# Attention outputs kept once and split on return, returns on another queue, and a tile's finish moved: a decoder layer on one core

## The chip, the cores and the metric

The kernel runs on one core of one Trainium2 chip. It is one launch, in fp32 at its inputs and outputs. The metric is the device time of that launch in microseconds (us), as the median of its runs; lower is better. PE is TensorE (the matrix engine), DVE is VectorE, ACT is ScalarE, POOL is GpSimd, SP is SyncE, which here only issues transfers.

## The reference

One decoder layer: 512 tokens, width 2048, 16 query heads of 128 in 4 key/value groups, a feed-forward width of 5632.

```python
hn = rmsnorm(x, mix_norm_g)
h  = x + nsa_mixer(hn, ...)                       # attention in three branches
h  = h + swiglu(rmsnorm(h, ffn_norm_g), ffn_w_in, ffn_w_out)
return rmsnorm(h, final_norm_g)

# nsa_mixer, for each head:
proj = hn @ w_in                                  # q, and k and v for three branches, and gates
s_c  = q @ kcc.T + bias;  o_c = softmax(s_c) @ vcc    # 31 compressed keys (an MLP over 32-token blocks)
s_s  = q @ k_sel.T + bias; o_s = softmax(s_s) @ v_sel # chosen blocks of 64 keys
s_w  = q @ k_win.T + bias; o_w = softmax(s_w) @ v_win # window of 512
o    = gate_c * o_c + gate_s * o_s + gate_w * o_w
return concat(o) @ w_out
```

All softmaxes are causal. With 512 tokens there are only 8 blocks and up to 16 may be chosen, so the chosen branch covers every earlier key, and the window covers them too.

## The kernel before

Every fp32 product is made of three products of rounded pieces: a value is kept as a high piece (ACT copies it to the rounded type) and a low piece (DVE subtracts the high piece from the value). `three` (lines 266 to 269) issues high x high, high x low and low x high; which of L267, L268 and L269 a row has tells which of the three it is.

**Weights.** The class `Weights` brings them as granules of 128x1024. `load` (L81) issues the transfer into one of three buffers `raw`; `split` makes `whi` (ACT, L97) and `wlo` (DVE, L98); `take` hands out a granule and keeps three more split ahead. `W.queue` is POOL's queue while attention runs, and SP's before and behind it.

**Stages.** Up to about 200 us the kernel normalises the input, projects the first keys, values and queries and builds the compressed keys. From 200 to 705 us attention runs. Behind it come the rest of the output projection, the second norm and the feed-forward network to the end of the span at 2136 us.

**Attention** is a loop over 16 heads (h), of 12 steps (i) each, written out by hand; each engine executes its instructions in the order in which this loop issues them. Four kinds of work are interleaved:

- `scores(h+1, t)`, at i = 2, 5, 8 and 11 for the token tiles t = 3, 2, 1, 0 of the next head: PE's products into `s`, DVE's addition of the bias with a running minimum (L791, three per tile), ACT's exponentials (L793).
- `finish(h+1, t)`, at i = 3, 6, 9 and at step 0 of the next head: DVE scales the probabilities by gate over sum (reciprocal L798, products L805) and transposes them in blocks of 32 (L806); SP issues four transfers `d_p<-p` to DRAM (L808).
- `fetch(t)`: SP brings the turned probabilities back, `ptr<-d_p` (L812). It stands at i = 8 for tiles 3 and 2, and at steps 0 and 3 of the next head for tiles 1 and 0.
- `turn(h, b, kt)`, at steps 0 to 8, splits one piece of the fetched probabilities into `pth` (ACT, L829) and `ptl` (DVE, L833; L831 for the compressed branch). `values` two steps later multiplies it by the values into `o` (L267 to L269; L844 for the compressed branch, at step 10).

`head_out`, at step 10, splits `o` into `of0` and `of1` and stores both pieces in DRAM for heads 0 to 11, two transfers `d_o<-of`; heads 12 to 15 are split straight into `hn_h` and `hn_l`. These two tiles hold the normalised input until the last projection has read it, and take the heads' outputs then.

**The dense stream** fills PE between these: `dense` yields projections of queries (`qpair`), keys and values for later heads, and then four `partial` products of the first twelve heads' outputs with `w_out`, each ending in a sum with the input (`stage<-in_x`, L702) that goes to DRAM (`d_h<-stage`, L718). Each yield stands for 6 products and counts as 650 ns. `pump(h, step)` advances the stream until its count has reached a goal for this step:

```python
goal = 20800 * min(at, 13) + 18300 * max(at - 13, 0)
```

During the last query pair, `reload_o` (L694 to L697) brings the twelve heads' outputs back into `hn_h` and `hn_l`: six transfers of 1 MB on SP's queue, two for each four heads, as each quarter of the normalised input has been read. The partial products read them as they are; a later stage multiplies the rest of `w_out` with all sixteen heads.

Of the kernel before, what the change touches and what calls it, by code (L numbers as in the profile page):

```python
# [10 lines left out]
F32 = mybir.dt.float32  # L11
# [162 lines left out]
def nsa_block(ctx: ExitStack, tc: tile.TileContext, x, rel_bias, mix_g, ffn_g, fin_g, w_in, w_out,  # L174
# [21 lines left out]
    d_t = dram.tile([H, UL], F32, name="d_t")  # L196
    d_u = dram.tile([128, H * UL], F32, name="d_u")
    d_c = dram.tile([H, 16 * CL], F32, name="d_c")
    d_o = dram.tile([12, 2, 128, S], F32, name="d_o")
    d_h = dram.tile([S, 256 * N_SPILL], F32, name="d_h")  # L200
    d_r = dram.tile([NT, 128, D], F32, name="d_r")
    d_a = dram.tile([NF // 2, 128, 2 * S], F32, name="d_a")
# [87 lines left out]
    def split_from(psum_ap, hi, lo, scale=None):  # L290
        if scale is None:
            act(hi, psum_ap, AF.Copy)
            dve.tensor_tensor(lo, psum_ap, hi.bitcast(F32), op=OP.subtract)
        else:
            act(hi, psum_ap, AF.Copy, scale=scale)
            dve.scalar_tensor_tensor(lo, psum_ap, scale, hi.bitcast(F32), op0=OP.mult, op1=OP.subtract)
# [333 lines left out]
    with ExitStack() as st2:  # L630
# [24 lines left out]
        def qpair(h0):  # L655
            ps = proj2()
            end = q_out(ps, h0)
            for i in range(4):
                yield from ws(ps, i, W.take(), end=end)
                if h0 == H - 2 and i < 3:  # L660
                    reload_o(i)
            done["n"] += 1
            yield None

# [27 lines left out]
            yield None  # L692

        def reload_o(i):  # L694
            for part, t in enumerate((hn_h, hn_l)):
                nc.sync.dma_start(t[:, 4 * i:4 * i + 4].bitcast(F32),
                                  d_o[4 * i:4 * i + 4, part].rearrange("h p s -> p h s"))  # L697

        def partial(cb):
            st = stage_tile().rearrange("p (t c) -> p t c", t=NT)  # L700
            c = slice(256 * cb, 256 * (cb + 1))
            nc.sync.dma_start(st, x[:, c].rearrange("(t p) c -> p t c", p=128))  # L702
            ps = [p.rearrange("p (t c) -> p t c", t=2) for p in proj2()]
            for i in range(3):
                w = W.take()
                for t in range(NT):
                    if i == 2 and t == 2:
                        W.ahead(3)
                    for k in range(4):
                        h = 4 * i + k  # L710
                        three(ps[t // 2][:, t % 2], hn_h[:, h, tok(t)], hn_l[:, h, tok(t)], w[0][:, k], w[1][:, k],
                              h == 0 and t % 2 == 0, h == 11)
                        if k % 2:
                            yield 650
                    if i == 2 and t % 2:
                        b = t // 2
                        dve.tensor_tensor(st[:, 2 * b:2 * b + 2], st[:, 2 * b:2 * b + 2], ps[b], op=OP.add)
            nc.sync.dma_start(d_h[:, c].rearrange("(t p) c -> p t c", p=128), st)  # L718
            done["n"] += 1
            yield None  # L720

# [13 lines left out]

        def pump(h, step):
            at = h + (step + 4) / STEPS
            goal = 20800 * min(at, 13) + 18300 * max(at - 13, 0)
            while done["ns"] < goal:
                c = next(stream, "end")  # L740
                if c == "end":
                    return
                done["ns"] += c or 0
# [52 lines left out]
        def finish(h, t):  # L796
            r = HS[h]["sm"][:, t]
            dve.reciprocal(r, r)  # L798
            dve.tensor_mul(r, r, gates[:, t, h])
            for i, p in enumerate(HS[h].pop(t)):  # L800
                o = p
                if not i:
                    o = P[t][:, :3, runs[t] - 32:]
                    p = CX[t].unsqueeze(1).to_broadcast([128, 3, 32])
                dve.tensor_scalar(o, p, r[:, i:i + 1], None, op0=OP.mult)  # L805
            dve.transpose(P[t], P[t])  # L806
            for i in range(4):
                nc.sync.dma_start(d_p[t][:, :, i].rearrange("j a r -> a j r"), P[t][32 * i:32 * (i + 1)])  # L808

        def fetch(t):  # L810

            nc.sync.dma_start(PT[:, :, PT_STEP * t:PT_STEP * t + runs[t]], d_p[t].rearrange("j a i r -> (j a) i r"))  # L812
# [6 lines left out]
        def turn(h, b, kt):  # L819
            n = S - 128 * kt  # L820
            th = ap_.tile([128, 512], F32R, name="pth", bufs=3)
            tl = ap_.tile([128, 512], F32R, name="ptl")
            rows = 128 if b >= 0 else 96
            if b < 0:
                src = arrived(rows, 64, 0, PT_STEP + 64)
            else:
                src = arrived(rows, PT_STEP * kt + 32 * (kt + 1) * b + 32 * kt, kt, PT_STEP + 32 * b)
            th4, tl4 = (x[:rows, :n].rearrange("p (t i s) -> p t i s", i=4, s=32) for x in (th, tl))
            act(th4, src, AF.Copy)  # L829
            if b < 0:  # L830
                dve.tensor_tensor(th4[32:64], src[32:64], th4[32:64].bitcast(F32), op=OP.subtract)  # L831
            else:
                dve.tensor_tensor(tl4, src, th4.bitcast(F32), op=OP.subtract)  # L833
            HS[h]["t", b, kt] = th[:rows, :n], tl[:rows, :n]
# [14 lines left out]
        def head_out(h):  # L849
            o = HS[h]["o"]  # L850
            if h < 12:
                f = [ap_.tile([128, S], F32R, name=f"of{i}", bufs=1) for i in range(2)]
                split_from(o, *f)
                for i in range(2):
                    nc.sync.dma_start(d_o[h, i], f[i].bitcast(F32))
            else:
                split_from(o, hn_h[:, h], hn_l[:, h])
            del HS[h]
# [11 lines left out]
        for h in range(H):  # L870
            seq = [(b, kt) for kt in (3, 2, 1, 0) for b in (0, 1)] + [(-1, 0)]
            for i in range(STEPS):
                if i == 4:
                    load_bias(h + 2)
                if i in (0, 3):
                    fetch(1 - i // 3)
                if i < 9:
                    turn(h, *seq[i])
                if i == 8 and h + 1 < H:
                    fetch(3)  # L880
                    fetch(2)
                if i == 0:
                    finish(h, 0)
                if h + 1 < H:
                    if i == 2:
                        drain_to(needed(h + 1))
                    if i % 3 == 2:
                        scores(h + 1, 3 - i // 3)
                    elif i % 3 == 0 and i:
                        finish(h + 1, 4 - i // 3)  # L890
                if 2 <= i < 11:
                    if i == 2 and h % HPG == 0:
                        drain_to(h)
                    values(h, *seq[i - 2])
                    if i == 10:
                        head_out(h)
                pump(h, i)
        W.queue = nc.sync
# [591 lines left out]
```

## Time and profile before

| | |
|---|---|
| median of 3 runs | 2136.5 us (2135.11 to 2139.32) |
| the profiled execution's own time | 2137.68 us |
| its span in the profile | 2136.0 us |
| mean granted TensorE clock | 0.996 |
| PE busy | 2103.2 us, 98% |
| DVE busy | 1634.8 us, 77% |
| ACT busy | 922.9 us, 43% |
| POOL busy | 118.2 us, 6% |
| bytes moved | 394.37 MB, 185 GB/s |

The span is the stretch that the profile covers, from the first to the last instruction. Busy time of an engine is the time in which it executes; matmuls overlap one another, so a row's duration of a matmul is longer than the distance to the next one. The granted clock is the share of full speed at which TensorE was allowed to run. A row of the timeline has the start in us, the duration in us, the engine, the line in the kernel, the operation, what is written from what (by the program's names), the shapes, and in square brackets the engine's idle time ahead of it and what ended that.

### The profile page before, as it was taken

The page shows a single profiled execution, that of the slowest core. Times are in us where ns is not written, and L with a number is a line of the kernel's source. Part 1 is how long each engine was busy: PE and PEld are TensorE (multiplying, and loading weights), DVE is VectorE, ACT ScalarE, POOL GpSimd, SP SyncE. Part 2 cuts the span into 40 slices and gives each one's busy share as a digit, 9 for nine tenths or more (in the row PEclk, how much of TensorE's full clock was granted, in tenths as well). Part 3 has the DMA queues.
Part 4 walks back from the last instruction along what each step waited for, and adds up shares of the span by engine and source line. Part 5 has one row for each costly group of instructions (what it writes and reads, how often), then busy time and mean ns, then how long its engine had stood idle before and what let it go on. Part 6 is the DMA issues. An engine that isn't in the chain of part 4 may idle for free.

```text
span 2136.0 us, 37198 instructions
## 1 busy us (share of the span) xinstructions
PE 2103.2 (98%) x14697; PEld 1949.5 (91%) x14697; DVE 1634.8 (77%) x2680; ACT 922.9 (43%) x1433; POOL 118.2 (6%) x195
## 2 busy tenths in 40 slices
PE   9999999999998999999999999999999999999998
PEld 7898788898988889899999999999999888999996
DVE  5565777878776357898888888888888787877785
ACT  5344454555544234444444343443434444544344
POOL 1000111111100000000000000000000000001000
PEclk9999999999999999999999999999999999999999
DMA  7555777776787643344434344433344776878894
GB/s 226 174 158 149 195 203 202 194 209 197 207 295 211 218 137 111 118 130 128 129 126 122 122 126 129 129 119 125 123 129 129 256 278 220 299 268 308 307 336 143
DMA packets 279147, 394.37 MB, mean 185 GB/s; under 512 B 34763, under 2 KB 208891, under 8 KB 278332
## 3 DMA queue, kind: packets, MB, share of 16 engines
q1 hardware_dynamic: 255324, 289.68, 43.5%
q0 software_dynamic: 21744, 98.12, 13.3%
q10 hardware_dynamic: 1904, 4.20, 0.5%
q8 instruction: 115, 1.88, 0.4%
q14 instruction: 60, 0.49, 0.1%
HBM read 323.67 MB, written 73.50 MB: 186 GB/s over the span
## 4 chain that ended last, share of the span: by engine, by line
PE 87%; DVE 5%; DMA 4%; ACT 2%; issue 2%; SPq 1%; POOL 0%; ACTq 0%; DVEq 0%; POOLq 0%
PE f L268 19%; PE f L269 19%; PE f L267 19%; PE proj L267 7%; PE proj L268 6%; PE proj L269 6%; DMA d_p<-p 1%; DVE wlo L98 1%; DMA ptr<-d_p 1%; PE pp L269 1%; PE pp L268 1%; PE pp L267 1%; PE po L269 1%; PE po L267 1%; PE po L268 1%
## 5 line engine op out<-in xcount | busy, mean ns | idle before, releaser
L98 DVE TENSOR_TENSOR wlo<-raw,whi 128x1024 fp32r<-128x1024 f32 (+1 forms) x226 | 270.6, 1200 | 117.2 <-ACT whi L97 116.7
L97 ACT ACTIVATE whi<-raw 128x1024 fp32r<-128x1024 f32 (+1 forms) x226 | 234.4, 1040 | 230.4 <-DVE raw L989 124.7
L989 DVE TENSOR_TENSOR tlo<-tt,thi 128x1536 fp32r<-128x1536 f32 (+2 forms) x135 | 197.1, 1460 | 110.1 <-ACT thi L1091 89.1
L267 PE MATMUL f<-hn_h,whi 128*128 128x256 f32 x984 | 271.7, 276 | 0.8 <-ACT E L1049 0.8
L269 PE MATMUL f<-hn_h,wlo 128*128 128x256 f32 x984 | 271.6, 276 | 0.0
L268 PE MATMUL f<-hn_l,whi 128*128 128x256 f32 x984 | 271.6, 276 | 0.0
L1086 ACT ACTIVATE whi<-raw 128x1024 fp32r<-128x1024 f32 x123 | 126.1, 1057 | 292.2 <-DVE raw L989 281.9
L267 PE MATMUL proj<-hn_h,whi 128*128 128x512 f32 x512 | 204.1, 399 | 0.5 <-ACT hn_h L402 0.5
L268 PE MATMUL proj<-hn_l,whi 128*128 128x512 f32 x512 | 200.7, 392 | 0.3 <-DVE hn_l L403 0.3
L269 PE MATMUL proj<-hn_h,wlo 128*128 128x512 f32 x512 | 200.9, 392 | 0.0
L267 PEld LDWEIGHTS f<-hn_h,whi 128*128 128x128 f32 x984 | 184.7, 188 | 1.2 <-ACT E L1049 1.2
L269 PEld LDWEIGHTS f<-hn_h,wlo 128*128 128x128 f32 x984 | 184.7, 188 | 0.0
L268 PEld LDWEIGHTS f<-hn_l,whi 128*128 128x128 f32 x984 | 184.7, 188 | 0.0
L1091 ACT ACTIVATE thi<-tt 128x1536 fp32r<-128x1536 f32 x82 | 121.8, 1486 | 84.8 <-PE f L268 75.3
L989 DVE TENSOR_TENSOR wlo<-raw,whi 128x1024 fp32r<-128x1024 f32 x123 | 147.0, 1223 | 0.0
L267 PE MATMUL proj<-whi,hn_h 128*128 128x256 f32 (+2 forms) x496 | 146.7, 296 | 0.0
L269 PE MATMUL proj<-whi,hn_l 128*128 128x256 f32 (+2 forms) x496 | 146.0, 294 | 0.0
L268 PE MATMUL proj<-wlo,hn_h 128*128 128x256 f32 (+2 forms) x496 | 145.9, 294 | 0.0
L269 PE MATMUL f<-whi,tlo 128*128 128x512 f32 x320 | 124.9, 390 | 0.6 <-DVE tlo L989 0.6
L268 PE MATMUL f<-wlo,thi 128*128 128x512 f32 x320 | 125.0, 391 | 0.0
L267 PE MATMUL f<-whi,thi 128*128 128x512 f32 x320 | 124.7, 390 | 0.0
L269 PEld LDWEIGHTS proj<-hn_h,wlo 128*128 128x128 f32 x512 | 96.5, 189 | 21.5 <-DVE wlo L98 0.2
(323 smaller groups left out, 6087.1 us busy)
## 6 DMA issues: line engine op xcount, KB each, us to landing
raw<-in_ffn_w_in SPq DMA_DIRECT2D x135, 512.0 KB, 3.8
raw<-in_ffn_w_out SPq DMA_DIRECT2D x88, 512.0 KB, 5.7
rawx<-in_ffn_w_in SPq DMA_DIRECT2D x41, 512.0 KB, 4.8
rawx<-d_a SPq DMA_DIRECT2D x31, 512.0 KB, 5.2
ah<-d_s POOLq DMA_DIRECT2D x16, 896.0 KB, 7.0
al<-d_s POOLq DMA_DIRECT2D x16, 896.0 KB, 9.5
raw<-in_nsa_w_in SPq DMA_DIRECT2D x24, 512.0 KB, 5.1
raw<-in_nsa_w_in POOLq DMA_DIRECT2D x24, 512.0 KB, 4.7
```

The source lines that it names most:

```text
L97: self.nc.scalar.activation(hi[:, :n], src, AF.Copy)
L98: self.nc.vector.tensor_tensor(lo[:, :n], src, hi[:, :n].bitcast(F32), op=OP.subtract)
L267: mm(o, ah, bh, start=start, stop=False, skip_group_check=True)
L268: mm(o, ah, bl, start=False, stop=False, skip_group_check=True)
L269: mm(o, al, bh, start=False, stop=stop, skip_group_check=True)
L989: dve.tensor_tensor(o, a, b, op=OP.subtract)
L1086: act(h, r, AF.Copy)
L1091: act(h, ttf, AF.Copy)
```

## The change

- `d_o` holds one fp32 piece per head. `head_out` copies `o` to `of` on ACT and stores it with one transfer; DVE's subtraction there is gone.
- `reload_o` brings three times 1 MB, all into `hn_l`, on POOL's queue. A new `split_o(k)` splits two heads at a time: ACT copies `hn_l` to `hn_h`, DVE subtracts in place. Heads 0 to 3 (k = 0, 1) are split behind quarters 2 and 3 of the last query pair, the other eight (k = 2 to 5) inside the first partial product.
- In `partial`, `stage<-in_x` and `d_h<-stage` go to POOL's queue, the first of them behind the second granule instead of ahead of the first.
- The stream's goal behind head 13 grows by 22500 per head, not 18300.
- `ptl` gets its own count of three buffers (the pool's own count before).
- The fetch of tile 1 moves from step 0 to step 1; the fetch of tile 2 for the next head from step 8 to step 10.
- `finish(h+1, ·)` stands at steps 5, 8 and 11, straight behind the next tile's scores, where it stood at steps 3, 6 and 9. The last tile's finish stays at step 0 of the next head.
- The compressed branch's product and `head_out` move from step 10 to step 11.

```diff
-    d_o = dram.tile([12, 2, 128, S], F32, name="d_o")
+    d_o = dram.tile([12, 128, S], F32, name="d_o")
...
                 if h0 == H - 2 and i < 3:
                     reload_o(i)
+                if h0 == H - 2 and i > 1:
+                    split_o(i - 2)
...
         def reload_o(i):
-            for part, t in enumerate((hn_h, hn_l)):
-                nc.sync.dma_start(t[:, 4 * i:4 * i + 4].bitcast(F32),
-                                  d_o[4 * i:4 * i + 4, part].rearrange("h p s -> p h s"))
+            pool.dma_start(hn_l[:, 4 * i:4 * i + 4].bitcast(F32), d_o[4 * i:4 * i + 4].rearrange("h p s -> p h s"))
+
+        def split_o(k):
+            h, l = (x[:, 2 * k:2 * k + 2] for x in (hn_h, hn_l))
+            act(h, l.bitcast(F32), AF.Copy)
+            dve.tensor_tensor(l, l.bitcast(F32), h.bitcast(F32), op=OP.subtract)
...
         def partial(cb):
...
-            nc.sync.dma_start(st, x[:, c].rearrange("(t p) c -> p t c", p=128))
...
                 w = W.take()
+                if i == 1:
+                    pool.dma_start(st, x[:, c].rearrange("(t p) c -> p t c", p=128))
                 for t in range(NT):
+                    if not cb and i < 2 and t % 2 == 0:
+                        split_o(2 + 2 * i + t // 2)
...
-            nc.sync.dma_start(d_h[:, c].rearrange("(t p) c -> p t c", p=128), st)
+            pool.dma_start(d_h[:, c].rearrange("(t p) c -> p t c", p=128), st)
...
-            goal = 20800 * min(at, 13) + 18300 * max(at - 13, 0)
+            goal = 20800 * min(at, 13) + 22500 * max(at - 13, 0)
...
-            tl = ap_.tile([128, 512], F32R, name="ptl")
+            tl = ap_.tile([128, 512], F32R, name="ptl", bufs=3)
...
             if h < 12:
-                f = [ap_.tile([128, S], F32R, name=f"of{i}", bufs=1) for i in range(2)]
-                split_from(o, *f)
-                for i in range(2):
-                    nc.sync.dma_start(d_o[h, i], f[i].bitcast(F32))
+                f = ap_.tile([128, S], F32, name="of", bufs=1)
+                act(f, o, AF.Copy)
+                nc.sync.dma_start(d_o[h], f)
...
-                if i in (0, 3):
+                if i in (1, 3):
                     fetch(1 - i // 3)
                 if i < 9:
                     turn(h, *seq[i])
                 if i == 8 and h + 1 < H:
                     fetch(3)
+                if i == 10 and h + 1 < H:
                     fetch(2)
...
                     if i % 3 == 2:
                         scores(h + 1, 3 - i // 3)
-                    elif i % 3 == 0 and i:
-                        finish(h + 1, 4 - i // 3)
-                if 2 <= i < 11:
+                        if i > 2:
+                            finish(h + 1, 4 - i // 3)
+                if 2 <= i < 10 or i == 11:
...
-                    values(h, *seq[i - 2])
-                    if i == 10:
+                    values(h, *seq[min(i - 2, 8)])
+                    if i == 11:
                         head_out(h)
```

## The prediction

> **What bounds the kernel now.** I read the page first, then the busy time by stretches of 50 us, then the gaps of PE in the timeline, then what DVE, ACT and SP did around those gaps.
>
> ```profile
> span 2136.0 us, 37198 instructions
> ...
> PE 2103.2 (98%) x14697; PEld 1949.5 (91%) x14697; DVE 1634.8 (77%) x2680; ACT 922.9 (43%) x1433; POOL 118.2 (6%) x195
> ```
>
> PE is busy 98% of the span: 32.8 us are idle. The change adds and removes no matmul, it only moves one kind by a step, so the new time is the same PE work plus whatever idle time and slow clock are left. The question is where the 32.8 us are.
>
> ```profile
> 200.00:250.00 50.00, 43.23 (x200) 35.02 (x199) 36.25 (x105) 22.63 (x61) 4.50 (x6) 0.97 0.62 168
> ...
> 600.00:650.00 50.00, 45.56 (x328) 42.67 (x326) 35.51 (x98) 20.98 (x57) 4.50 (x6) 0.97 0.82 276
> 650.00:700.00 50.00, 44.85 (x336) 42.68 (x337) 32.18 (x83) 19.82 (x49) 4.35 (x6) 0.97 0.67 200
> 700.00:750.00 50.00, 50.00 (x255) 42.69 (x254) 16.71 (x17) 12.36 (x13) 0.70 (x1) 1.00 0.61 218
> ...
> sum 301.20, PE 299.48 PEld 263.93 DVE 239.47 ACT 154.15 POOL 44.42; mean PE 29.95 PEld 26.39 DVE 23.95 ACT 15.41 POOL 4.44
> ```
>
> The columns are length, then PE, PEld, DVE, ACT and POOL busy, then granted clock and DMA. Attention (200 to 705 us) holds over half of the idle time: 6.8 us at its start, 4.4 and 5.2 us at its end, and, by the sum over ten heads in the middle (276.4 to 577.6 us), only 1.7 us in 301 us. Behind 700 us PE is full, so what attention gives back, the end of the kernel gains.
>
> ```profile
> 222.32 0.30 PE L267 MATMUL o<-pth,v0h 128*128 128x128 f32 x1 [2.51 <-issue]
> 234.26 0.44 PE L268 MATMUL o<-ptl,v0h 128*128 128x384 f32 x1 [1.84 <-DVE ptl L833]
> 366.77 0.50 PE L844 MATMUL o<-pth,vcc 96*128 96x512 f32 x1 [0.37 <-DVE pth L831]
> 608.79 0.50 PE L844 MATMUL o<-pth,vcc 96*128 96x512 f32 x1 [1.33 <-DVE pth L831]
> 620.01 0.33 PE L267 MATMUL o<-pth,v1h 128*128 128x128 f32 x1 [2.73 <-ACT pth L829]
> 650.66 0.33 PE L267 MATMUL o<-pth,v1h 128*128 128x128 f32 x1 [1.04 <-ACT pth L829]
> 663.29 0.44 PE L268 MATMUL o<-ptl,v1h 128*128 128x384 f32 x1 [2.26 <-DVE ptl L833]
> 690.39 0.44 PE L267 MATMUL o<-pth,v1h 128*128 128x384 f32 x1 [1.83 <-ACT pth L829]
> ```
>
> All of these are value products (o) that wait for their turned probabilities, pth and ptl. A gap also costs clock behind it:
>
> ```profile
> 620.00:624.00 4.00, 3.98 (x19) 3.85 (x20) 3.88 (x13) 1.73 (x5) 0.59 (x1) 0.57 0.52 155
> ```
>
> Granted clock 0.57 over 4 us: 0.43 x 4 = 1.7 us lost. The 0.97 in three of the stretches above is one such dip each (0.03 x 50 = 1.5 us): behind the gaps at 234, 620 and 690. [...]
>
> Attention therefore loses 6.8 + 2 + 4.4 + 5.2 = 18.4 us of idle time and three dips of 1.7 us: 23.5 us. Why the late gaps exist:
>
> ```profile
> 619.65 0.31 ACT L829 ACTIVATE pth<-ptr 128x128 fp32r<-128x128 f32 x1 [4.04 <-DMA ptr<-d_p]
> ...
> 689.81 0.94 ACT L829 ACTIVATE pth<-ptr 128x384 fp32r<-128x384 f32 x2 [7.28 <-DMA ptr<-d_p]
> ...
> 605.95 0.62 SPq L696 DMA_DIRECT2D hn_l<-d_o  x1
> 608.77 3.05 SPq L812 DMA_DIRECT2D ptr<-d_p  x2
> ...
> SPq L702 <- DMA d_h<-stage: 10.1, 3, 4.4
> ```
>
> ptr is the fetch of turned probabilities. At 608.77 two fetches stand on SP's queue right behind two returns of 1 MB each, and land 10.8 us later. SP also stood still for 10.1 us at line 702, with the probabilities' DMAs behind it.
>
> **The change part by part.**
>
> *Half the return, on POOL.* Twelve stores of 256 KB and three returns of 1 MB fall away (6 MB), and 12 DVE subtractions (line 293, of). The stores hide behind everything already. The three returns that are left stand on POOL's queue behind and ahead of weight loads; they wait for PE's reads of the piece they overwrite, which SP did before without loss, and the weights behind them are split three granules (over 15 us) ahead of use. At the fetches, SP no longer holds the returns or line 702's wait, so the 4.0 and 7.3 us that ACT waited should fall to little. [...]
>
> *Finish behind the next scores.* Every head had three places like this:
>
> ```profile
> 590.83 0.42 DVE L833 TENSOR_TENSOR ptl<-ptr,pth 128x256 fp32r<-128x256 f32 x1 [1.33 <-ACT pth L829]
> 591.17 0.17 DVE L798 RECIPROCAL sm<-sm 128x3 f32<-128x3 f32 x1
> ...
> 593.99 1.18 DVE L98 TENSOR_TENSOR wlo<-raw,whi 128x1024 fp32r<-128x1024 f32 x1
> ```
>
> DVE waits 1.3 us for ACT, which is still exponentiating, and then finishes the tile in 2.8 us (591.17 to 593.99). With the finish straight behind the scores, ACT works meanwhile. Two such waits per head go (2.7 us) and one subtraction of 0.65 us. DVE's busy 23.95 us in 30.1 was tight only because of these waits; PE's 0.17 us per head goes, also because L844 moves from step 10 to 11. Gain 1.7 us. In head 0 the ptl on which PE waited 1.84 us at 234.26 stood behind a finish of 2.8 us that now runs later; against that its fetch is issued behind one more set of stores, about 2.9 us later. I keep 0.3 us of that gap, and half of its dip: gain 1.5 + 0.85 = 2.4 us (bounds 0 and 3.5).
>
> *What the finish loses.* A finished tile's stores start 2 steps (5 us) later in the head, and the fetch of tile 2 moves from step 8 to 10. It must close a loop within one head of 30.1 us:
>
> ```profile
> d_p<-p SPq DMA_DIRECT2D x64, 112.0 KB, 2.1
> ptr<-d_p SPq DMA_DIRECT2D x16, 448.0 KB, 6.7
> ...
> ptr<-d_p SPq DMA_DIRECT2D x16, 320.0 KB, 3.4
> ```
>
> Counting DVE's new order from the moment PE ends a head's last scores, finish(2) of the next round ends at 28.7 us; the fourth store is issued 1.5 us later and lands in 2.1: 32.3. The fetch takes 3.4 us by the tile that was fetched alone and 6.7 by this tile when it stood right behind the 576 KB one; alone I take 4.7 (3.4 x 448/320). ptr at 37.1, its turning done at 37.9; DVE then is free for the scores of tile 2 about 1.0 us before PE brings them. So the loop closes, cost 0, with about 1 us to spare.
>
> *Splitting on return.* Six ACT copies and six DVE subtractions of 128x1024, each priced like a weight's (1.04 and 1.18 us). Five have time. split_o(1) has none: PE's stream goes from the last query pair straight to the first partial product, which reads heads 2 and 3 in its second pair. The rows of before around this place:
>
> ```profile
> 593.61 0.29 PE L267 MATMUL s<-k1h,qh 128*128 128x288 f32 x1
> 605.18 0.28 PE L267 MATMUL proj<-whi,hn_h 128*128 128x256 f32 x1
> 605.30 0.28 PE L268 MATMUL proj<-wlo,hn_h 128*128 128x256 f32 x1
> ...
> 596.03 0.18 DVE L791 CUSTOM_DVE_ANT_0 cx<-s,biasc 128x31 f32<-128x31 f32 x1
> 599.74 0.69 DVE L833 TENSOR_TENSOR ptl<-ptr,pth 128x512 fp32r<-128x512 f32 x1 [2.56 <-ACT pth L829]
> 600.35 0.17 DVE L798 RECIPROCAL sm<-sm 128x3 f32<-128x3 f32 x1
> 602.77 1.18 DVE L98 TENSOR_TENSOR wlo<-raw,whi 128x1024 fp32r<-128x1024 f32 x1
> 608.77 0.19 DVE L791 CUSTOM_DVE_ANT_0 cx<-s,biasc 128x31 f32<-128x31 f32 x1
> 609.57 0.69 DVE L319 SCALAR_TENSOR_TENSOR yt<-proj,ybc 128x512 f32<-128x512 f32 x1
> 611.00 0.69 DVE L293 TENSOR_TENSOR ql<-yt,qh 128x512 fp32r<-128x512 f32 x1 [0.74 <-ACT qh L292]
> 605.73 1.04 ACT L97 ACTIVATE whi<-raw 128x1024 fp32r<-128x1024 f32 x1
> ```
>
> PE began the partial at 605.18, but DVE came to the pair's last half (yt) only at 609.57, 13.5 us behind the scores at 596.03. In the new order that stretch loses the idle 2.6 us, has a finish of 2.8 in place of one of 2.4 (600.35 to 602.77), gains split_o(0), 1.2 us, and a second finish of 2.4 us ahead of yt: 13.5 - 2.6 + 0.4 + 1.2 + 2.4 = 14.9 us. Caught up, DVE starts it at 594.8, as PE's scores (from 593.61, 1.1 us long) end, so yt is at 609.7. Then yt to qh 1.3, the copy 1.05, the subtraction 1.2: heads 2 and 3 are ready at 613.2. PE wants them at 605.18 + 6 x 0.12 = 605.9, at the pitch of the rows 605.18 and 605.30. It stands 7.3 us, and a dip of 1.7 us behind it. Bounds: below, PE's gap is nothing if DVE is already through; above, 10 us if the copies also queue behind exponentials. I take 7.3, as every duration in it is a row. It replaces the 1.33 and 2.73 us and the dip at 608 to 624 (5.8 us): loss 3.2 us.
>
> *The pace of 22500.* The last head's compressed product stands here:
>
> ```profile
> 701.26 0.39 PE L844 MATMUL o<-pth,vcc 96*128 96x512 f32 x1
> ```
>
> Behind head 12 PE gets 210 short matmuls at that pitch per head where it had 168, by the order of the instructions: 24.8 us instead of 19.9, so with about 8 us of the head's own products a head lasts 33 us on PE, instead of 28, which DVE and the DMAs couldn't follow: from 608.79 to the last head's compressed product at 701.3, three heads took 30.8 us each. The gaps at 650, 663 and 690 and the last dip (1.04 + 2.26 + 1.83 + 1.7 = 6.8 us) have no ground left. The stream then runs out six steps early: four value groups and one product stand bare at the end of head 15, where the last fetch has to be in about 17 us behind its scores. That costs 0 to 2.5 us; I take 1.0. Gain 5.8 us.
>
> **Sum:** 2.4 + 1.7 - 3.2 + 5.8 = 6.7 us. The profiled execution took 2137.68 us with its span of 2136.0, so 2131.0 by its own clock; it lay 1.2 us above the median of the three runs (2136.5, from 2135.1 to 2139.3). Forecast 2130.0 us.
>
> **Rivals.**
>
> *The loop doesn't close (slower).* If the fetch of tile 2 lands 6.7 us behind its issue, as it did, and not 4.7, its turning ends 1.0 us past what the loop allows. DVE then starts each head's scores later than the head before, until o waits at step 2 or 3; some 3 us of slack go first, then about 1.1 us per head over 13 heads: 14 - 3 = 11 us, and the 1.7 us of the middle aren't won. 2130 + 12.7 = 2142.7. It decides from a fetch of about 5.7 us. For it: DVE 80% busy and the DMA engines at 0.6 to 0.8. Against: 6.7 was measured behind another fetch on the same queue.
>
> *The split stands wider (no change).* split_o(2) and (3) follow on ACT and DVE ahead of the next scores; if those hold up head 13 as well, or the returns on POOL land late, 4 to 6 us more: 2134 to 2136.
>
> *The split is covered (faster yet).* If DVE is some 7 us earlier at yt than I count, the gap and its dip vanish: 2130 - 9 = 2121.
>
> *The changed transfers don't matter.* If ptr's lateness came from the DMA engines' load and not from SP's order, one gap of 2.7 us and a dip stay in head 12 beside the split: 2134. Against: half the bytes go in any case.
>
> **How the numbers follow.** A measurement here can't tell less than 0.2% (4.3 us) from no change. Forecast 0.48 (2127 to 2133); split covered 0.14; loop open 0.22 (2136 to 2148); wider split or late transfers 0.16 (2133 to 2137). Faster by over 0.2% (below 2132.2): nearly all of the forecast's 0.48 and the 0.14, 0.60. Slower (above 2140.8): most of the loop's case, 0.18. Within: 0.22. The range from 2121.5 to 2143.0 takes in the covered split and the lower half of the open loop.
>
> **What would show it.** Right: in the middle heads no PE gap, DVE's waits for pth gone from behind the scores; one gap of 5 to 9 us at the first matmuls of the first partial product, waiting for hn_h or hn_l from the split lines, with the clock near 0.5 behind it; no o waiting for ptr in heads 13 to 15; PE idle in attention about 14 us. Wrong: o at steps 2 to 4 waiting in head after head with growing gaps (the open loop), or PE running through the first partial without a gap.

## The result and the profile after

The changed kernel takes 2141.8 us (median of 8 runs, 2139.98 to 2145.48) against 2136.6 us before (8 runs, 2134.92 to 2139.32): a ratio of 1.0026 (95% interval 1.0015 to 1.0037), 5.2 us slower. The forecast was 2130.0 us. The profiled execution took 2139.98 us with a span of 2138.3 us; it is the fastest of the eight, so its trace shows somewhat less loss than the median.

The page's head, and the stretches that answer to those of before (columns: length, PE, PEld, DVE, ACT and POOL busy, granted clock, DMA share, GB/s):

```profile
span 2138.3 us, 37128 instructions
...
PE 2102.9 (98%) x14697; PEld 1950.1 (91%) x14697; DVE 1636.3 (77%) x2674; ACT 934.0 (44%) x1439; POOL 127.1 (6%) x207
```

```profile
200.00:250.00 50.00, 44.96 (x209) 36.86 (x208) 37.34 (x111) 22.77 (x64) 4.50 (x6) 0.97 0.62 174
276.40:577.60 301.20, 297.37 (x1724) 261.86 (x1724) 230.54 (x640) 156.18 (x405) 43.00 (x58) 1.00 0.68 190
600.00:650.00 50.00, 42.66 (x307) 40.58 (x306) 39.87 (x93) 25.93 (x58) 5.25 (x7) 0.93 0.59 182
650.00:700.00 50.00, 50.00 (x412) 49.38 (x411) 34.46 (x93) 19.84 (x52) 9.56 (x13) 1.00 0.77 233
700.00:750.00 50.00, 47.27 (x199) 38.33 (x199) 17.57 (x21) 14.01 (x17) 1.47 (x2) 0.93 0.58 215
```

PE's idle time at attention's start fell from 6.8 to 5.0 us, and between 650 and 700 us from 5.2 to nothing: the second as forecast, the first by less. But the ten heads in the middle, which had 1.7 us of idle time, have 3.8; 600 to 650 us has 7.3 instead of 4.4; and a new loss stands at 700 us, 2.7 us idle. The two stretches at a clock of 0.93 lose 3.5 us each (0.07 x 50). The gaps of PE, in the timeline:

```profile
498.31 0.33 PE L268 MATMUL o<-ptl,v0h 128*128 128x128 f32 x1 [0.99 <-DVE ptl L841]
529.88 0.33 PE L268 MATMUL o<-ptl,v0h 128*128 128x128 f32 x1 [0.98 <-DVE ptl L841]
590.62 0.33 PE L268 MATMUL o<-ptl,v1h 128*128 128x128 f32 x1 [0.89 <-DVE ptl L841]
614.63 0.58 PE L267 MATMUL proj<-whi,hn_h 128*128 128x256 f32 x1 [6.87 <-ACT hn_h L701]
615.89 0.58 PE L269 MATMUL proj<-whi,hn_l 128*128 128x256 f32 x1 [0.47 <-DVE hn_l L702]
702.71 0.45 PE L267 MATMUL o<-pth,v1h 128*128 128x384 f32 x1 [1.59 <-ACT pth L837]
705.50 0.69 PE L268 MATMUL o<-ptl,v1h 128*128 128x384 f32 x1 [0.84 <-DVE ptl L841]
```

The stall at 614.63 is the one that the prediction expected at the first partial product. The rows ahead of it, about 1 us in every second or third head, and those at 702 us were not expected.

The idle time of the middle understates its loss: the rows of matmuls overlap (at 605.18 and 605.30 us before, 0.28 us long and 0.12 us apart), so a wait that is shorter than this overlap doesn't show as idle. From the compressed product of head 1 to that of head 11 both traces hold the same 1738 matmuls; they took 301.1 us before and 304.4 us in the changed kernel, 3.3 us longer.

What ACT waits for between 276.4 and 577 us, before and after (busy us and mean ns, then idle us ahead of the group and what ended it):

```profile
L793 ACT ACTIVATE p<-u,mx 128x256 f32<-128x256 f32 (+3 forms) x80 | 44.2, 554 | 3.2 <-ACT cx L793 2.5
...
L829 ACT ACTIVATE pth<-ptr 128x128 fp32r<-128x128 f32 (+4 forms) x90 | 40.9, 474 | 0.8 <-DMA ptr<-d_p 0.8
```

```profile
L801 ACT ACTIVATE p<-u,mx 128x128 f32<-128x128 f32 (+3 forms) x78 | 43.4, 557 | 24.5 <-DMA d_p<-p 20.7 <-ACT cx L801 2.0 <-DVE p L813 1.3
L837 ACT ACTIVATE pth<-ptr 128x128 fp32r<-128x128 f32 (+4 forms) x90 | 42.0, 477 | 34.1 <-DMA ptr<-d_p 31.4 <-PE s L269 2.7
```

The second fence is the changed kernel. Before, the exponentials waited for no transfer. Now they wait 20.7 us for `d_p<-p`, the stores of probabilities. They wait because there are two probability buffers for four tiles:

```python
two = [ap_.tile([128, 4 * runs[t]], F32, name=f"p{t}", bufs=1) for t in (2, 3)]
P = [two[t % 2][:, :4 * runs[t]].rearrange("p (j r) -> p j r", j=4) for t in range(NT)]
```

Tile 0's exponentials write the buffer of tile 2, so tile 2's four stores must have read it first. The waits for the fetch `ptr<-d_p` rose too, from 0.8 to 31.4 us. One such place, on DVE, SP, ACT and PE in turn:

```profile
518.29 1.11 DVE L814 STREAM_TRANSPOSE p<-p 128x896 f32<-128x896 f32 x1
519.43 2.72 SPq L816 DMA_DIRECT2D d_p<-p  x4
525.02 0.40 ACT L801 ACTIVATE p<-u,mx 128x128 f32<-128x128 f32 x1 [3.09 <-DMA d_p<-p]
526.61 0.29 DVE L841 TENSOR_TENSOR ptl<-ptr,pth 128x128 fp32r<-128x128 f32 x1 [2.49 <-ACT pth L837]
529.88 0.33 PE L268 MATMUL o<-ptl,v0h 128*128 128x128 f32 x1 [0.98 <-DVE ptl L841]
```

Tile 2's finish ends at 519.4, its stores are issued to 522.2 and have landed by 525.0. ACT stands for 3.09 us, takes up the next head's first pieces late, DVE waits 2.49 us for those, and PE 0.98 us for DVE. Before, that finish stood two steps (some 5 us) earlier, and the stores had that time.

### The profile page after: what moved, and what is told of

Read it like the earlier page. It is cut to its first block, busy times and chain, and to the rows that moved or that the text cites. A ratio compares the mean times of both kernels' runs of the same rounds, so it can differ in the third digit from the quotient of the medians.

```text
span 2138.3 us, 37128 instructions
## 1 busy us (share of the span) xinstructions
PE 2102.9 (98%) x14697; PEld 1950.1 (91%) x14697; DVE 1636.3 (77%) x2674; ACT 934.0 (44%) x1439; POOL 127.1 (6%) x207
## 4 chain that ended last, share of the span: by engine, by line
PE 78%; DVE 9%; DMA 6%; ACT 3%; issue 2%; SPq 2%; ACTq 0%; DVEq 0%
PE f L268 19%; PE f L267 19%; PE f L269 19%; PE proj L267 4%; PE proj L269 4%; PE proj L268 4%; DMA ptr<-d_p 3%; DMA d_p<-p 3%; SPq L816 2%; DVE wlo L98 2%; DVE p L813 1%; DVE ptl L841 1%; ACT whi L97 1%; PE pp L267 1%; PE pp L268 1%
```

## The experiments

Every kernel is compared with the kernel before in runs that lie beside its own. "First po" is the start, in the kernel's profile, of the first product behind attention, 710.4 us before and 712.9 us in the changed kernel: it holds all of attention, and with it what lies ahead of attention, which differs by up to 2 us between the profiles. "Ten heads" is the time from the compressed product of head 1 to that of head 11, the same 1738 matmuls in every profile. The last column is PE's idle time from 276.4 to 577.6 us.

| kernel | median us | ratio to before (95%) | first po | ten heads us | middle idle |
|---|---|---|---|---|---|
| before | 2136.6 | | 710.4 | 301.1 | 1.7 |
| changed | 2141.8 | 1.0026 (1.0015 to 1.0037) | 712.9 | 304.4 | 3.8 |
| e1 own buffer for tile 0 | 2143.3 | 1.0025 (1.0015 to 1.0034) | 714.4 | 301.7 | 1.1 |
| e2 old order | 2139.8 | 1.0019 (1.0008 to 1.0030) | 712.6 | 297.4 | 0.0 |
| e3 early split | 2141.8 | 1.0022 (1.0013 to 1.0031) | 715.2 | 306.9 | 6.3 |
| e4 pace 18300 | 2152.9 | 1.0070 (1.0057 to 1.0083) | 727.5 | 307.2 | 6.0 |
| e5 before + new order alone | 2159.2 | 1.0110 (1.0096 to 1.0125) | 727.9 | 308.1 | 7.6 |
| e6 no returns | 2139.6 | 1.0015 (1.0006 to 1.0023) | 713.2 | 305.1 | 5.2 |
| e7 old order, early split | 2136.5 | 0.9999 (0.9990 to 1.0008) | 708.3 | 297.6 | 0.0 |
| e8 as e7, returns on SP | 2127.5 | 0.9957 (0.9945 to 0.9970) | 700.1 | 297.6 | 0.0 |
| e9 returns on SP alone | 2144.1 | 1.0040 (1.0026 to 1.0054) | 716.1 | 303.9 | 4.5 |
| e10 as e8, new order | 2142.2 | 1.0030 (1.0019 to 1.0042) | 713.2 | 303.2 | 3.7 |
| e11 as e8, pace 18300 | 2130.6 | 0.9977 (0.9967 to 0.9987) | 703.7 | 297.7 | 0.0 |
| e12 as e8, heads 4 to 11 split late | 2126.5 | 0.9957 (0.9944 to 0.9969) | 699.7 | 297.5 | 0.0 |

Up to head 11 the changed kernel, e3, e4, e6 and e9 run the same instructions, and their ten heads took 303.9 to 307.2 us: differences of that size between two profiles of the new order are not an effect of the edit. With the old order (e2, e7, e8, e11, e12) the ten heads took 297.4 to 297.7 us.

**e1: is it the shared buffer?**

```diff
         two = [ap_.tile([128, 4 * runs[t]], F32, name=f"p{t}", bufs=1) for t in (2, 3)]
-        P = [two[t % 2][:, :4 * runs[t]].rearrange("p (j r) -> p j r", j=4) for t in range(NT)]
+        two += [ap_.tile([128, 4 * runs[t]], F32, name=f"p{t}", bufs=1) for t in [0]]
+        mine = {0: 0, 1: 1, 2: 0, 3: 1}
+        mine.update({t: 2 + i for i, t in enumerate([0])})
+        P = [two[mine[t]][:, :4 * runs[t]].rearrange("p (j r) -> p j r", j=4) for t in range(NT)]
...
-            tl = ap_.tile([128, 512], F32R, name="ptl", bufs=3)
+            tl = ap_.tile([128, 512], F32R, name="ptl")
```

> The changed kernel, but tile 0's probabilities get a buffer of their own instead of sharing tile 2's (for the room, ptl goes back to the pool's two buffers). In the trace of the changed kernel ACT stands 23.7 us between 276 and 590 us at the exponentials of p, released by the stores d_p<-p, and 32.7 us at pth, released by the fetch ptr<-d_p; before, 0 and 0.8 us. Theory A (the shared buffer: the late finish makes the last tile's exponentials wait for tile 2's stores, ACT comes late to pth, PE's o waits 1 us per head): the 23.7 us go to nearly nothing, PE's idle time from 276 to 590 us falls from about 4.7 us to below 1.5, time 2138 to 2139 us. Theory B (the fetch of tile 2 stands too late in the round, as the rival 'the loop doesn't close' had it): the 23.7 us go, but the wait at pth for ptr grows by as much, PE's 4.7 us stay, time 2141 to 2143 us.

```profile
L804 ACT ACTIVATE p<-u,mx 128x128 f32<-128x128 f32 (+3 forms) x80 | 44.2, 554 | 4.3 <-DMA d_p<-p 1.6 <-ACT cx L804 1.5 <-DVE mx L802 0.6
L840 ACT ACTIVATE pth<-ptr 128x128 fp32r<-128x128 f32 (+4 forms) x90 | 42.0, 477 | 53.8 <-DMA ptr<-d_p 47.6 <-PE o L267 4.1 <-PE o L269 1.6
```

(The expectation's 23.7 and 32.7 us were read to 590 us.) From 276 to 577 us the wait for the stores went from 20.7 to 1.6 us and PE's idle time to 1.1 us, as theory A had it. The waits for ptr rose from 31.4 to 47.6 us, as theory B had it, and PE still pays for them, in waits too short to show as idle: the ten heads took 301.7 us, 2.7 less than in the changed kernel (and 2.2 less than in the lowest of the five profiles) but 4.3 more than with the old order (e2 below). So the shared buffer is a part of the loss in the middle, and the late fetches that stand behind it are the likely rest. The two buffers of `ptl`, which e1 changes as well, are not told apart by a run; in its trace DVE waits 1.1 us in ten heads for PE to free them. The time did not fall: the profile has a new gap of 2.21 us and a dip at 591 us, 8.05 us at the first partial product and three dips' worth (5.1 us of clock, in part while PE stands) behind that.

**e2: the old order of the loop, everything else changed.** finish at 3, 6, 9, fetches at 0, 3, 8, the last product at 10.

> The changed kernel with the old order of the head loop alone: finish at steps 3, 6 and 9, fetches at steps 0, 3 and 8, the compressed product and head_out at step 10. Everything else stays changed. Theory A and theory B both: PE's idle time from 276 to 590 us falls from 4.7 to about 1.7 us, ACT's waits for d_p and ptr there to under 2 us. They and the tail: if the gaps of 1.59 and 0.84 us and the dip of 3.4 us at 700 to 711 us come from the late stores and fetches too, they go as well: 2141.8 - 3 - 5 + 1.8 (the gap at 234 us comes back) = 2135.5 us. If the tail comes from the pace alone, it stays: 2140.5 us. The stall of 7.3 us at the first partial product stays in either case.

Both waits of ACT are gone (the first group below waits for no transfer, the second 1.7 us), PE has no idle time in the middle, and from one compressed product to the next a head takes 29.7 us, where it took 30.1 before and 29.7 to 31.7 in the changed kernel. The ten heads took 297.4 us: the order costs 7.0 us there (304.4 in the changed kernel; 6.5 to 9.8 over the five profiles), and the other parts of the change gain 3.7 (301.1 before). The two gaps at 702 us are gone too, so they belong to the order, not to the pace.

```profile
L801 ACT ACTIVATE p<-u,mx 128x256 f32<-128x256 f32 (+3 forms) x82 | 45.2, 552 | 3.2 <-ACT cx L801 2.5
...
L837 ACT ACTIVATE pth<-ptr 128x128 fp32r<-128x128 f32 (+4 forms) x90 | 42.1, 475 | 6.3 <-PE o L269 4.5 <-DMA ptr<-d_p 1.7
```

Yet the time is only 2 us lower, and the two intervals overlap, because head 12 got worse (47.8 us from head 11's compressed product to head 12's, 40.3 in the changed kernel):

```profile
604.26 0.50 PE L267 MATMUL o<-pth,v1h 128*128 128x512 f32 x1 [3.84 <-ACT pth L837]
610.24 0.50 PE L268 MATMUL o<-ptl,v1h 128*128 128x512 f32 x1 [1.34 <-DVE ptl L841]
617.59 0.58 PE L267 MATMUL proj<-whi,hn_h 128*128 128x256 f32 x1 [5.92 <-ACT hn_h L701]
620.49 0.58 PE L269 MATMUL proj<-whi,hn_l 128*128 128x256 f32 x1 [2.10 <-DVE hn_l L702]
```

These are 13.2 us of gaps, and there are 6.8 us of lost clock, in part within the gaps. Two things stand there: a fetch that ACT had to wait 6.8 us for, and the split.

**e3: the split of heads 2 and 3 earlier, in the changed kernel.**

```diff
-                if h0 == H - 2 and i > 1:
-                    split_o(i - 2)
+                if h0 == H - 2 and i == 2:
+                    split_o(0)
+                    split_o(1)
```

> The changed kernel with split_o(1) (heads 2 and 3) issued together with split_o(0) behind the third granule of the last query pair, not behind its fourth. Theory S (PE's stall of 6.87 us at 614.63 us is nothing but split_o(1)'s place behind the query pair's endings on ACT and DVE): the stall and its dip go, 7.3 us of idle time and about 1.9 us of clock: 2132 to 2134 us. Rival (ACT and DVE are late as a whole there, so PE meets the next wait, split_o(2) or the next scores, instead): at most half of it comes back, 2137 to 2139 us.

The time is the changed kernel's, 2141.8 us. The stall shrank from 6.87 to 2.31 us, but from the compressed product of head 11 to that of head 13 the two profiles agree within half a microsecond, 72.5 us in the changed kernel and 72.1 in this one. Theory S's 8 to 10 us did not come. That ACT and DVE are late as a whole and PE meets the next wait instead, as the rival had it, fits, and is not shown: this profile has a gap of 2.27 us and a dip at 592 us, where the changed kernel's has 0.89 us and none, and that hides some of what the split gained. It also shows late stores beside a return: tile 2's four stores, issued from 583.3 us on beside the first return, held ACT for 5.88 us, and PE 2.27 us with a dip behind it.

```profile
591.10 0.40 ACT L802 ACTIVATE p<-u,mx 128x128 f32<-128x128 f32 x1 [5.88 <-DMA d_p<-p]
592.71 0.33 PE L267 MATMUL o<-pth,v1h 128*128 128x128 f32 x1 [2.27 <-ACT pth L838]
```

**e4: the old pace in the changed kernel** (`18300 * max(at - 13, 0)`).

> The changed kernel with the stream's goal behind head 13 back at 18300 per head. Theory P (22500 cures the gaps of heads 13 to 15, but leaves the last head bare): the gaps at 702 and 705 us and their dip go (4 to 5 us back), and gaps at o of 1 to 2.5 us each come back in heads 13 to 15 (5 to 7 us lost): 2142 to 2144 us. Rival (with the returns off SP's queue those gaps would be gone at either pace): only the tail's cost goes, 2137 us.

11 us slower than the changed kernel, far outside what either theory gave. From one compressed product to the next, heads 13 and 14 took 28.7 and 29.6 us and not 32.2 and 31.5: 5.4 us less, for 78 short matmuls less (336 instead of 414), which at 0.116 us each are 9.0 us of work. What is left over stands in the last head, 34.1 us instead of 24.2, and 36 matmuls behind it. So where PE has less to do, the loop in the new order sets the time. Not all of the 11 us is the pace's, as far as the profiles show: head 12's compressed product, up to which the two paces differ by at most 1.05 us of the stream's count, already stands 7.2 us later than in the changed kernel, with a gap of 2.90 us and two dips at 594 us ahead of it, and 7.5 us come behind it. What the pace alone costs stays open.

**e5: the new order alone, in the kernel before.**

> The kernel before with one part of the change alone: finish at steps 5, 8 and 11, fetch of tile 1 at step 1 and of tile 2 at step 10, the compressed product and head_out at step 11. Outputs, returns and pace stay as before. The prediction had this part as a gain of 1.7 us in the middle. Theory A (late stores hold the shared probability buffer and the fetches; the one-piece outputs are what gained in the middle): ACT's waits at p for d_p<-p and at pth for ptr appear from 276 to 577 us (together over 40 us), single heads take 31 to 32 us from one compressed product to the next, PE's idle time there rises from 1.7 to 4 to 8 us: 2140 to 2145 us. Rival (the order is harmless and the waits in the changed kernel come from the queues): 2135 us.

23 us slower than before, more than expected. Theory A's signs are all there: ACT waits 17.2 us for the stores and 23.5 us for ptr in the middle, PE's idle time there is 7.64 us, and single heads are up to 31.9 us long. The ten heads took 308.1 us, 7.1 more than before.

```profile
276.40:577.60 301.20, 293.56 (x1702) 258.63 (x1701) 234.67 (x646) 154.41 (x403) 42.58 (x57) 1.00 0.69 197
```

Most of the rest is behind 600 us: a gap of 5.71 us at 608 us and, in each of heads 13 to 15, about 3 us (2.92, 3.41, 3.14) with dips, at the old pace. This is the part that the prediction booked as a gain.

**e6: no returns.** The first twelve heads' outputs are left out of the result.

> The changed kernel without the three returns of 1 MB: it splits what hn_l holds from the projections, so the outputs of the first twelve heads are left out of its result; everything else runs. Theory C (the returns' bytes delay the stores and fetches of heads 11 and 12, whatever queue they are on: tile 2's stores took 5 us to land beside the first return): the gap at 591 us and its dip go, and ACT's waits for ptr and d_p from 580 to 625 us fall to the 2 to 4 us per head of the middle; the stall at the first partial product stays at 6 to 8 us since the splits keep their place: 2138 to 2140 us. Rival (the stall is the returns' landing): the stall goes too, 2131 us.

This is theory C's outcome: the stall at the first partial product is 6.96 us without a byte of return, so it is not a return's landing, and the splits' place on ACT and DVE is what is left; the gap at 591 us is 0.59 us and has no dip. Without any return the changed kernel is still 3.5 us slower than the kernel before.

**e7 and e8: old order, splits earlier, and then the returns back on SP.**

```diff
-                yield from ws(ps, i, W.take(), end=end)
+                for n, y in enumerate(ws(ps, i, W.take(), end=end)):
+                    if h0 == H - 2 and i == 3 and n == 3:
+                        split_o(2)
+                        split_o(3)
+                    yield y
...
+                if h0 == H - 2 and i == 2:
+                    split_o(0)
+                    split_o(1)
...
-                    if not cb and i < 2 and t % 2 == 0:
-                        split_o(2 + 2 * i + t // 2)
+                    if not cb and i == 0 and t % 2 == 0:
+                        split_o(4 + t // 2)
# e8 also:
-            pool.dma_start(hn_l[:, 4 * i:4 * i + 4]...
+            nc.sync.dma_start(hn_l[:, 4 * i:4 * i + 4]...
```

Both have the head loop's old order, as e2.

> As e2_finish_back (old order of the head loop, everything else changed), and the splits moved: heads 0 to 3 behind the third granule of the last query pair, heads 4 to 7 in the middle of its fourth, heads 8 to 11 in the first partial product. e2's profile lost in head 12: 3.84 and 1.34 us at o (fetch late), 5.92 and 2.10 us at the first partial products (split late), and two dips. Theory S: the 5.92 and 2.10 us and the second dip go: 2139.8 - 10 = 2129 to 2131 us. Rival (ACT and DVE are held by the late fetch, the splits queue behind it): half of it, 2134 to 2136 us.

> As e7_back_and_early, with the returns on SP's queue instead of POOL's. Theory C (bytes, not the queue): the fetches of head 12 stand directly behind 1 MB and are as late or later, 0 to 3 us slower than e7. Rival (on POOL's queue the returns run beside the fetch and take its share, on SP's they would be through ahead of it; and POOL's weights no longer stand behind a return that waits for a store): 2 to 5 us faster than e7.

e7 took away the stalls at the split but not the late fetch: 3.93, 2.18 and 1.40 us of gaps at o and five dips' worth of clock (8.5 us) in head 12. e8 differs from it by the queue of three transfers and is 9 us faster, against theory C. Transfers from 583 to 603 us, e7 and then e8 (KB each, median us from issue to landing):

```profile
hn_l<-d_o POOLq DMA_DIRECT2D x2, 1024.0 KB, 8.3
...
ptr<-d_p SPq DMA_DIRECT2D x1, 320.0 KB, 5.5
...
d_p<-p SPq DMA_DIRECT2D x4, 48.0 KB, 7.5
ptr<-d_p SPq DMA_DIRECT2D x1, 192.0 KB, 7.6
```

```profile
hn_l<-d_o SPq DMA_DIRECT2D x3, 1024.0 KB, 7.8
...
d_p<-p SPq DMA_DIRECT2D x3, 48.0 KB, 4.6
```

On POOL's queue the returns start at 577.65, 584.89 (as PE has read its quarter) and 592.55 us, the later two beside tile 0's stores (584.83) and tile 0's fetch (593.83), which waits for these stores to land. On SP's queue they start behind the stores that stand ahead of them, at 584.10, 591.55 and 599.04 us, and tile 0's fetch had gone out at 588.66, between the first two. In e7 ACT and PE wait for that fetch:

```profile
593.83 0.53 SPq L825 DMA_DIRECT2D ptr<-d_p  x1
601.53 0.63 ACT L842 ACTIVATE pth<-ptr 128x512 fp32r<-128x512 f32 x1 [6.30 <-DMA ptr<-d_p]
602.21 0.79 PE L267 MATMUL o<-pth,v1h 128*128 128x512 f32 x1 [3.93 <-ACT pth L842]
```

In e8 ACT waits for no fetch in head 12:

```profile
588.66 0.54 SPq L825 DMA_DIRECT2D ptr<-d_p  x1
593.26 0.61 ACT L842 ACTIVATE pth<-ptr 128x512 fp32r<-128x512 f32 x1
```

What is left in e8 behind the first heads is one gap of 3.61 us at 607.5 us, the compressed product behind two splits on DVE, and smaller ones of 1.1 and 0.8 us.

**e9: the returns on SP in the changed kernel.**

> The changed kernel with the three returns on SP's queue, as before; nothing else. With the old order of the head loop and early splits the queue alone was worth 9 us (e7 to e8). Theory Q (on POOL's queue a return starts as soon as PE has read its quarter, and the small stores and fetches on SP's queue land late beside it; on SP's queue it waits its turn): the late stores at 583 to 592 us and the gap and dip there go, time not above the run without any return: 2136 to 2140 us. Rival (in the new order stores and fetches are issued so late that on SP's queue they stand behind 1 MB each time): 2142 to 2146 us.

No gain: the interval overlaps the changed kernel's. In the new order the fetches of tiles 1 and 0 go out at 591.78 us, between two returns at 591.30 and 593.12, and ACT waits 5.38 us for the first of them; PE's gap of 2.01 us at 600.55 us follows. The queue paid only with the old order (and the earlier splits of e7 and e8).

**e10: e8 with the new order.**

> e8_back_early_sp with the order of the head loop as the change has it (finish at 5, 8, 11; fetches at 1, 3, 8, 10; last product and head_out at 11). It prices the order beside one-piece outputs without the other costs. Theory A: the middle's idle time of 0.0 becomes 4 to 6 us, the last head's gaps and dip at 702 us come back (4 to 5 us), one or two dips more: 2127.5 + 10 = 2136 to 2140 us. Rival (the order only hurt through the returns): 2128 to 2130 us.

2142.2 us: the order alone costs 14.7 us here. By the heads' distances in the two profiles, 6.2 us from head 0's compressed product to head 11's (333.6 us against 327.4), 4.1 in heads 12 and 13, and 2.3 in the last head, where the gaps at 703 and 706 us and the dip of 3.4 are back. One late head of e10, and the same head of e8:

```profile
487.78 0.40 PE L857 MATMUL o<-pth,vcc 96*128 96x512 f32 x1
518.83 0.40 PE L857 MATMUL o<-pth,vcc 96*128 96x512 f32 x1
```

```profile
484.32 0.46 PE L857 MATMUL o<-pth,vcc 96*128 96x512 f32 x1
514.08 0.40 PE L857 MATMUL o<-pth,vcc 96*128 96x512 f32 x1
```

31.05 us against 29.76.

**e11 and e12: the pace, and the place of the later splits, in e8.**

> e8_back_early_sp with the stream's pace behind head 13 back at 18300. Theory P (with 56 groups of products per head, 19.5 us, and some 8 us of its own a head is shorter on PE than the 29.7 us that the loop takes, and PE stands for the rest; with 70 groups it is full): about 2 us per head in heads 13 and 14 and a longer bare last head: 2131 to 2135 us. Rival (the pace only moves where the same work stands): 2127 to 2129 us.

> e8_back_early_sp with heads 4 to 7 split where the change has them, at the first and third token tile of the first partial product's first granule, and heads 8 to 11 in its second; only heads 0 to 3 stay early. In e8's profile DVE came 3.61 us late to the compressed product at 607.5 us, behind two splits (2.36 us) and a dip of 1.7 followed. Theory D (DVE's queue is the bound of this stretch): that gap falls to about 1.3 us and the dip goes, 1 to 1.5 us come back at the second granule: 2125 to 2127 us. Rival (the stall moves whole to the second granule, as in e3, 2 to 3 us with a dip): 2127 to 2130 us.

The pace of 22500 is worth 3 to 4 us in the old order (2130.6 us without it, 3.0 by the medians and 0.2% by the ratios): a wait of 2.85 us for the last head's fetch and smaller ones come back at 18300, as theory P had it. Heads 13 and 14, with 168 short matmuls each, took 30.6 and 28.1 us, so in the old order the loop can go at 28.1 us. e12 takes late splits for heads 4 to 11: the gap at the compressed product falls to 1.33 us, 1.54 and 0.76 us come up at the second granule, and one dip stays; 2126.5 us, not told apart from e8 but as good. e8 and e12 take 0.43% less than the kernel before (8.4 to 8.6 us by the medians), and are faster than the changed kernel by more.

## Why the prediction was wrong

*What the finish loses: cost 0.* This is the step that failed. I followed one loop, the fetch of tile 2. The fetch itself was well sized: 4.7 us was taken for it and its median in the changed kernel is 4.1 us.

```profile
ptr<-d_p SPq DMA_DIRECT2D x10, 448.0 KB, 4.1
```

The stores ahead of it were not: 3.6 us was counted from the end of the finish to the landing, and at the place shown it took 5.6 (519.43 to 525.02), more than the 1 us to spare. And the other reader of a finished tile I left out: the next tile that is written into the same buffer. The two buffers were in the code, and the stores' time and their place were in the sum, but not the wait that they put on ACT two steps later. The ten middle heads took 3.3 us longer where I had a gain of 1.7; against e2, which differs by the order alone, they took 7.0 longer, of which e1 gets 2.7 back by a buffer of its own. The rival "the loop doesn't close" had the sign and nearly the size (2142.7 us). Its link, the late fetch, is not the one that came first here, but it is the wait that is left in e1.

*Finish behind the next scores: gain.* This failed as well. Two waits of DVE for pth per head were to go; from 276.4 to 577.6 us there are 30 of them in both kernels, and they became longer (us in total, times, longest; before, then the changed kernel):

```profile
DVE ptl L833 <- ACT pth L829: 38.0, 30, 1.4
DVE ptl L841 <- ACT pth L837: 43.5, 30, 2.5
```

The middle did have something to win, 3.7 us, but e2 wins it with the old order; so it is the subtraction and the store that went, or the third buffer of `ptl`, which all stayed in e2 and which no run takes apart.

*Start.* 1.7 us of idle time went (2.4 forecast): the wait at 234 us is gone, but its dip now follows the gap at 222 us.

*The first partial product.* Right: 7.3 us and a dip of 1.7 forecast, 6.87 + 0.47 us measured, with 3.4 us of clock lost, about half of which falls on idle time. e6 rules out that it is a return's landing. The gap it should have replaced went, as forecast.

*The pace.* Right for the gaps at 650, 663 and 690 us. Mis-sized at the end: 1.0 us was taken for the bare last head, and it cost 2.4 us of gaps and 3.4 us of clock in place of the dip that went. e2 and e8, at the same pace with the old order, have nothing over 0.3 us and 0.8 us there, and e10 brings the gaps back, so it is once more the order: tile 1's fetch, issued at 694.85 us behind tile 0's stores and together with tile 0's fetch, took 7.2 us to land, and ACT waited 6.64 us for it. The middle and the last head, 5.0 and 4.8 us short of their terms, are about what the profiles lack of the forecast (9.0 us: 6.7 to be gained, 2.3 lost).

*Half the return, on POOL.* Wrong that the fetches would be on time beside a return: with the old order this cost 9 us (e7 to e8). Whether SP's order or the returns' bytes had held the fetches before is not told apart: in e8 the returns, at half the bytes, stand on SP again, and ACT waits for no fetch in head 12. e7's fetch of 192 KB, issued at 593.83 us, 1.28 us behind the third return on POOL's queue, took 7.6 us, 2.6 times the 2.9 us that this fetch took in the middle heads of e8. What held it up no run shows, nor that this fetch is the whole of the 9 us.

*What stays open.* The profiles of before and after differ by 2.3 us of span, the medians by 5.2: the profiled execution of the changed kernel lacks the dip at 592 us that three other kernels with its order show (e1, e3, e4, gaps of 2.2 to 2.9 us; e3 and e4 run the same instructions up to there). That this is what the median has more is likely, and not shown. The order cost 23 us alone, 2 us beside the other changes and 15 us in e10. In the ten middle heads it cost much the same each time, 7.1, 7.0 and 5.7 us; the difference is made behind head 11, where against the changed kernel e2 loses some 4 us, by a late fetch and the split, and e5 loses 10.8 us against the kernel before.

## What to carry to other kernels

When a step is moved later, follow every reader of what it frees as well as every reader of what it makes: a buffer that two tiles share turns a later store into an earlier wait of the next writer. A large transfer on a queue of its own was not out of the way here: placed in order behind the small urgent ones, on their queue, it cost 9 us less (e7 and e8, with the old order). And undo parts from both sides, since with several waits in a row taking one away shows almost nothing (2 us for the order, nothing for the split) until the others are gone. Idle time alone is no measure either: the distance between two fixed instructions with the same work between them showed 7.0 us where idle time showed 3.8.

## What the runs showed of the hardware that was not expected

Lost clock came in steps. In the profiles of before and after, the clock of every dip between 200 and 750 us stood at 0.50, for 3.41 us or twice that (620.55 to 623.96 us before; 612.04 to 618.87 and 704.20 to 711.03 us in the changed kernel): 1.70 or 3.4 us lost. e1 lost 5.1 us behind its gap of 8.05 us, and e7 8.5 us in head 12, three and five times 1.70. So several gaps of 1.4 to 3.9 us within some 15 us cost more clock (e7) than one of 8.05 us (e1). A gap's length alone did not settle it: dips followed gaps of 1.83 us (before, at 690 us) and of 1.54 and 0.76 us (e12, at 611 and 613 us), and none followed the gap of 2.26 us at 663 us (before: a clock of 1.00 from there to 690 us).

Stores and fetches landed late beside a large transfer on another queue: in e7 four stores of 48 KB in 7.5 us and a fetch of 192 KB in 7.6 us, against 3.4 and 2.9 us in the middle heads of e8. It is not so every time: in the changed kernel, with its returns on POOL's queue too, the 48 KB stores of that stretch (583 to 603 us) landed in 1.8 us and the 192 KB fetch in 7.2.
